# Forward substitution of the 32x32 inverses: from VectorE to GpSimd, its negation and transposed copy to ScalarE

## The chip, the cores and the metric

The kernel runs on one core of a Trainium2 chip. The metric is device time in microseconds of one execution, given as the median of several runs. The core has five engines that work side by side, each through a queue of its own in an order fixed when the kernel is built: TensorE (PE in the profile; PEld is its weight load), VectorE (DVE), ScalarE (ACT), GpSimd (POOL) and SyncE (SP), which issues most of the transfers. They meet at semaphores only.

## The reference, cut to what matters

One layer of a hybrid decoder: 512 prompt tokens and 8 x 8 sampled tokens (576 columns), 1024 channels. After a norm and a combined projection, a Mamba-2 branch and an RWKV-7 branch run side by side; then come an output projection, a SwiGLU block and a gated embedding. The change lies in RWKV-7, whose state obeys, token by token and head by head,

```
s_kk = einsum('bhvk,bhk->bhv', s, kk_t)
s = (s * w_t[:, :, None, :] - s_kk[..., None] * (kk_t * a_t)[:, :, None, :]
     + v_t[..., None] * k_t[:, :, None, :])
out = einsum('bhvk,bhk->bhv', s, r_t)
```

The kernel doesn't step through tokens. It takes 64 tokens as a group; within a group the dependence of each token on the earlier ones is a strictly triangular 64x64 matrix L for each head, and the group is solved with the inverse of (I + L).

## The kernel before

The 576 columns make nine groups of 64 tokens (group 0 holds the sampled tokens). The 16 heads are done in four quarters of four heads. For a quarter, `prep` makes the decayed keys and queries, `gram` makes the triangular matrices (`Lst`) with TensorE and masks them, `solve` and `combine` invert them, `chain` walks through the groups with the 64x64 state, and `head_norm` finishes the output. Quarters overlap: while the chain of one quarter runs, the next is prepared and inverted, and the fourth inverse is traced after the early loads of the Mamba-2 branch.

`solve` (L652 to L679) inverts the two 32x32 diagonal blocks of every 64x64 matrix: 2 blocks x 2 heads of a pair x 18 (9 groups, 2 pairs) = 72 blocks for a quarter. Four transfers (L662) write the blocks of `Lst` to DRAM, one (L665) brings them back as the tile `L`, one block to a partition: 72 partitions x 32 x 32. Then VectorE makes `Tt = -L` (L667), adds 1 on the diagonal (L668) and runs the substitution: for jx = 1 to 30 an outer product of row jx of L with column jx of `Tt` into `tmp` (L674), jx(31-jx) elements a partition, and a subtraction from the rest of `Tt` (L676). L677 writes the transposed copy of the first 36 blocks over `L`. L678 and L679 store `Tt` and the copy to DRAM (`Td`, `Ad`). `combine` loads them in another layout (L688, L690), and with two series of 32x32 matmuls (L698, L712) makes the off-diagonal block, so that the tile `TT` holds the 64x64 inverses. In `chain`, `core` uses `TT` at L797, between two small copies on ScalarE and VectorE (L791/L792 to `xs`, L804/L805 to `suv`); `prompt_state` updates the state at L831.

Beside this stand the projections ("fill"): all weights come in blocks of 128x512 in float32, are loaded by SyncE (L199, tile `raw`, three buffers) and split into a high and a low part, `whi` by ScalarE (L203, shown at the helper's line L93) and `wlo` by a subtraction (L206) that alternates between GpSimd and VectorE; each part has two buffers. TensorE does three products for every block (L221, L222, L223). A projected tile is then evacuated and worked on by ScalarE and VectorE: `shifted` (L368 to L371), `conved` (L395 to L401), `zed` (L411).

The order of each queue is not written by hand in these parts: the framework schedules instructions when the program is closed, by their place in the program text (earlier is more urgent) and a simulated timeline, and writes one fixed order for each engine. A few places are pinned (`issue_after`).

`V`, `S`, `G`, `T` are VectorE, ScalarE, GpSimd and TensorE; `act` is an activation on ScalarE, by default a copy with a scale.

Of the kernel before, what the change touches and what calls it, by code (L numbers as in the profile page):

```python
# [11 lines left out]
ALU = mybir.AluOpType  # L12
# [63 lines left out]
def hybrid_step(ctx, tc, A):  # L76
    nc = tc.nc
    V, S, G, T = nc.vector, nc.scalar, nc.gpsimd, nc.tensor
# [9 lines left out]
    def nm(s):  # L88
        uid[0] += 1
        return f"{s}_{uid[0]}"  # L90

    def act(out, in_, func=AF.Copy, scale=1.0, bias=0.0):
        return S.activation(out, in_, func, bias=bias, scale=scale)  # L93
# [80 lines left out]
    at, n = PV["shift_mu"]  # L174
    V.tensor_scalar(omu[:], pv[:, at:at + n], -1.0, 1.0, ALU.mult, ALU.add)
    hka = const("hka", [P, 16])
    at, n = PV["k_a"]
# [100 lines left out]
    def cslot(name, shape=None, dt=F32):  # L278
        return sp.tile(shape or [P, NT], dt, tag="cv", name=nm(name), bufs=3)
# [372 lines left out]
    def solve(s):  # L652

        q = s.q
        Ld = dp.tile([2, 2, 18, 32, 32], F32, tag=f"Ld{q}", name=f"Ld{q}")
        s.Td = dp.tile([2, 2, 18, 32, 32], F32, tag=f"Td{q}", name=f"Td{q}")
        s.Ad = dp.tile([2, 18, 32, 32], F32, tag=f"Ad{q}", name=f"Ad{q}")
        NB = 72
        for z in range(2):
            for e in range(2):  # L660
                r0 = e * 64 + z * 32
                nc.sync.dma_start(Ld[z, e].rearrange("g s t -> s g t"),  # L662
                                  s.Lst[r0:r0 + 32, :, :, z * 32:z * 32 + 32].rearrange("s g j t -> s (g j) t"))
        L = sp.tile([NB, 32, 32], F32, tag="L", name=nm("L"))
        nc.sync.dma_start(L[:], Ld[:].rearrange("z e g s t -> (z e g) s t"))  # L665
        Tt = s2.tile([NB, 32, 32], F32, tag="Tt", name=nm("Tt"))
        V.tensor_scalar(Tt[:], L[:], -1.0, None, ALU.mult)  # L667
        V.tensor_tensor(Tt[:].rearrange("p s t -> p (s t)")[:, 0:1024:33],  # L668
                        Tt[:].rearrange("p s t -> p (s t)")[:, 0:1024:33], ones[0:NB, 0:32], ALU.add)
        tmp = s2.tile([NB, 256], F32, tag="tmp", name=nm("tmp"))  # L670
        for jx in range(1, 31):
            n = 31 - jx
            o = tmp[:, 0:jx * n].rearrange("p (s t) -> p s t", s=jx)
            V.tensor_tensor(o, L[:, jx:jx + 1, jx + 1:32].to_broadcast([NB, jx, n]),  # L674
                            Tt[:, 0:jx, jx:jx + 1].to_broadcast([NB, jx, n]), ALU.mult)
            V.tensor_tensor(Tt[:, 0:jx, jx + 1:32], Tt[:, 0:jx, jx + 1:32], o, ALU.subtract)  # L676
        V.tensor_copy(L[0:36], Tt[0:36].rearrange("p s t -> p t s"))  # L677
        nc.sync.dma_start(s.Td[:].rearrange("z e g s t -> (z e g) s t"), Tt[:])  # L678
        nc.sync.dma_start(s.Ad[:].rearrange("e g s t -> (e g) s t"), L[0:36])  # L679

# [240 lines left out]
    def inverse(s):  # L921
        solve(s)
        fill_at(s, 7)
        combine(s)
# [331 lines left out]
    for what in SEQ:  # L1256
# [7 lines left out]
        elif what == "y":  # L1264
            for j in range(6):
                t = cslot("yl")
                nc.sync.dma_start(t[:], yr_d[j][:])
                YR.append(split(t[:], xp, ("xhi", "xlo"), [P, NT], lo_eng=G))
        else:
            ps = lin_ps()  # L1270
            linear(YR[0:6], ps)
            t = cslot("pr")
# [71 lines left out]
    def ft(name):  # L1344
        return pools[-1].tile([P, NT], F32, tag="f", name=nm(name), bufs=9 if len(pools) > 1 else 6)
# [31 lines left out]
    for k in range(4):  # L1377
        xa, xb, t = ft("xa"), ft("xb"), ft("tt")
# [100 lines left out]
    for a, b in ((0, 320), (320, NT)):  # L1479
        n = b - a  # L1480
# [17 lines left out]
        for c in range(8):  # L1498
# [14 lines left out]
            t = ft("pg")[:, 0:n]  # L1513
# [159 lines left out]
```

## Time and profile before

| | us |
|---|---|
| median of 3 runs | 1345.34 |
| lowest and highest of them | 1345.02, 1348.39 |
| span of the profiled execution, first to last instruction | 1349.0 |
| PE busy in the span | 1246.8 |
| DVE busy | 826.0 |
| POOL busy | 625.6 |
| ACT busy | 618.9 |

The profiled execution is one by itself; for it the profile gives the span alone, which lies 3.7 us above the median of the runs. In the profile's rows a line begins with the place in the kernel, the engine and the operation, then what is written and read, the shapes (partitions x elements a partition) and the count; after the bar stand the busy time in us, the mean of one in ns, and the idle time of the engine just before, with what ended most of it. In rows by time the first two numbers are the start and the duration in us, and a bracket gives the idle time before and what ended it. Rows of one line give minimum/median/maximum in ns. Matmul records are pipelined, so that their durations overlap.

### The profile page before, as it was taken

The page shows a single profiled execution, that of the slowest core. Times are in us where ns is not written, and L with a number is a line of the kernel's source. Part 1 is how long each engine was busy: PE and PEld are TensorE (multiplying, and loading weights), DVE is VectorE, ACT ScalarE, POOL GpSimd, SP SyncE. Part 2 cuts the span into 40 slices and gives each one's busy share as a digit, 9 for nine tenths or more (in the row PEclk, how much of TensorE's full clock was granted, in tenths as well). Part 3 has the DMA queues.
Part 4 walks back from the last instruction along what each step waited for, and adds up shares of the span by engine and source line. Part 5 has one row for each costly group of instructions (what it writes and reads, how often), then busy time and mean ns, then how long its engine had stood idle before and what let it go on. Part 6 is the DMA issues. An engine that isn't in the chain of part 4 may idle for free.

```text
span 1349.0 us, 26596 instructions
## 1 busy us (share of the span) xinstructions
PE 1246.8 (92%) x10525; PEld 1150.7 (85%) x10525; DVE 826.0 (61%) x1443; ACT 618.9 (46%) x1256; POOL 625.6 (46%) x597
## 2 busy tenths in 40 slices
PE   6897999999989978899999969989999999999997
PEld 6787897889868957788779859889999999999997
DVE  6648666887687785943466667886553135443454
ACT  6565436534654463343434364464442124433363
POOL 5425413642355154122456645565654336654642
PEclk9897799899979978889989989998999999999998
DMA  5322242234232412262454542222323222314322
GB/s 164 125 68 66 77 117 63 85 103 116 75 99 78 109 41 80 94 214 83 157 176 131 179 125 72 73 93 88 92 88 87 79 86 82 93 59 149 96 89 71
DMA packets 94461, 135.58 MB, mean 100 GB/s; under 512 B 34705, under 2 KB 39057, under 8 KB 94337
## 3 DMA queue, kind: packets, MB, share of 16 engines
q1 hardware_dynamic: 93760, 133.36, 32.4%
q8 instruction: 83, 1.36, 0.4%
q10 hardware_dynamic: 576, 0.52, 0.1%
q14 instruction: 42, 0.34, 0.1%
HBM read 106.10 MB, written 27.75 MB: 99 GB/s over the span
## 4 chain that ended last, share of the span: by engine, by line
PE 63%; DVE 14%; ACT 4%; issue 4%; DMA 3%; POOL 3%; DVEq 0%; SPq 0%; ACTq 0%; POOLq 0%
PE lin L234 21%; PE lin L1403 8%; PE lin L223 6%; PE lin L221 6%; PE lin L222 6%; DVE h L395 2%; PE lin L1508 1%; PE lin L1509 1%; PE lin L1510 1%; DVE tmp L674 1%; DVE wlo L206 1%; DVE Tt L676 1%; PE lin L613 1%; PE cx L797 1%; DVE suv L831 1%
## 5 line engine op out<-in xcount | busy, mean ns | idle before, releaser
L206 POOL TENSOR_TENSOR wlo<-raw,whi 128x512 fp32r<-128x512 f32 (+1 forms) x108 | 146.4, 1356 | 352.5 <-ACT whi L93 269.5
L93 ACT ACTIVATE whi<-raw 128x512 fp32r<-128x512 f32 (+1 forms) x232 | 143.3, 618 | 259.1 <-PE lin L234 126.4
L221 PE MATMUL lin<-xhi,whi 128*128 128x288 f32 (+1 forms) x784 | 243.3, 311 | 2.5 <-ACT whi L93 2.2
L223 PE MATMUL lin<-xhi,wlo 128*128 128x288 f32 (+1 forms) x784 | 241.5, 308 | 2.3 <-POOL wlo L206 2.3
L222 PE MATMUL lin<-xlo,whi 128*128 128x288 f32 (+1 forms) x784 | 241.5, 308 | 0.3 <-POOL xlo L194 0.3
L206 DVE TENSOR_TENSOR wlo<-raw,whi 128x512 fp32r<-128x512 f32 (+1 forms) x124 | 100.9, 814 | 103.2 <-PE lin L234 60.4
L221 PEld LDWEIGHTS lin<-xhi,whi 128*128 128x128 f32 (+1 forms) x784 | 151.0, 193 | 9.3 <-ACT whi L93 2.6
L223 PEld LDWEIGHTS lin<-xhi,wlo 128*128 128x128 f32 (+1 forms) x784 | 150.7, 192 | 6.2 <-POOL wlo L206 2.8
L222 PEld LDWEIGHTS lin<-xlo,whi 128*128 128x128 f32 (+1 forms) x784 | 150.8, 192 | 4.8 <-issue 1.2
L234 PE MATMUL lin<-xhi,whi 128*128 128x288 f32 x384 | 62.3, 297 | 3.2 <-ACT xhi L93 3.0
L234 PE MATMUL lin<-xlo,whi 128*128 128x288 f32 x384 | 60.8, 298 | 0.0
L234 PE MATMUL lin<-xhi,wlo 128*128 128x288 f32 x384 | 59.3, 297 | 0.0
L234 PEld LDWEIGHTS lin<-xhi,whi 128*128 128x128 f32 x384 | 54.6, 189 | 3.8 <-ACT xhi L93 1.7
L234 PEld LDWEIGHTS lin<-xlo,whi 128*128 128x128 f32 x384 | 54.8, 191 | 0.0
L234 PE MATMUL lin<-ah,wlo 128*128 128x288 f32 x352 | 54.7, 296 | 0.0
L234 PE MATMUL lin<-al,whi 128*128 128x288 f32 x352 | 54.7, 296 | 0.0
L234 PE MATMUL lin<-ah,whi 128*128 128x288 f32 x352 | 54.7, 296 | 0.0
L234 PEld LDWEIGHTS lin<-xhi,wlo 128*128 128x128 f32 x384 | 54.3, 191 | 0.0
L1403 PE MATMUL lin<-T,wh 128*128 128x288 f32 x320 | 50.1, 296 | 4.5 <-DVE T L194 2.8
L674 DVE TENSOR_TENSOR tmp<-L,Tt 72x30 f32<-72x30 f32 (+14 forms) x120 | 49.2, 410 | 3.2
L234 PEld LDWEIGHTS lin<-ah,whi 128*128 128x128 f32 x352 | 49.6, 189 | 0.0
L234 PEld LDWEIGHTS lin<-ah,wlo 128*128 128x128 f32 x352 | 49.6, 189 | 0.0
(425 smaller groups left out, 3197.8 us busy)
## 6 DMA issues: line engine op xcount, KB each, us to landing
raw<-wts SPq DMA_DIRECT2D x271, 256.0 KB, 2.6
S<-s_wkv SPq DMA_DIRECT2D x8, 512.0 KB, 5.1
hd<-s_ssm SPq DMA_DIRECT2D x8, 512.0 KB, 4.5
o_ssm_s<-hd SPq DMA_DIRECT2D x8, 512.0 KB, 2.9
xbc_d<-E SPq DMA_DIRECT2D x12, 288.0 KB, 2.1
x<-xT SPq DMA_DIRECT2D x8, 288.0 KB
gate_d<-g SPq DMA_DIRECT2D x8, 288.0 KB, 2.5
bv_d<-rw SPq DMA_DIRECT2D x8, 288.0 KB
```

Of the source, the lines that this page charges most:

```text
L93: return S.activation(out, in_, func, bias=bias, scale=scale)
L206: eng.tensor_tensor(lo[:, 0:n], raw[:, 0:n], hi[:, 0:n].bitcast(F32), ALU.subtract)
L221: T.matmul(ps[:, a:b], whi, xhi[:, a:b], start=first, stop=False)
L222: T.matmul(ps[:, a:b], whi, xlo[:, a:b], start=False, stop=False)
L223: T.matmul(ps[:, a:b], wlo, xhi[:, a:b], start=False, stop=last)
L234: T.matmul(ps[:, a:e], (hi, lo)[p][:, i * P:(i + 1) * P], xs[k + i][q][:, a:e], start=n == k + i == 0, stop=n == 2 and k + i == nk - 1, sk ...
L395: V.scalar_tensor_tensor(h[:], E[:, i:i + 600], w(i), h[:], ALU.mult, ALU.add)
L613: T.matmul(ps[:, c:c + 128].rearrange("p (a t) -> p a t", a=2), s.BK[jj][H[e], g].rearrange("p a t -> p (a t)"), s.G[H[e], g, jj, :, e], s ...
L674: V.tensor_tensor(o, L[:, jx:jx + 1, jx + 1:32].to_broadcast([NB, jx, n]), Tt[:, 0:jx, jx:jx + 1].to_broadcast([NB, jx, n]), ALU.mult)
L676: V.tensor_tensor(Tt[:, 0:jx, jx + 1:32], Tt[:, 0:jx, jx + 1:32], o, ALU.subtract)
L797: T.matmul(uw[H[e], jj, :], TT[H[e], g, jj, :], xs[H[e], jj, :], start=True, stop=True)
L1403: T.matmul(ps, (hi, lo)[p][:, k * P:(k + 1) * P], OPS[n][k][q], start=first and p == q == k == 0, stop=p == 1 and k == 3, skip_group_check ...
```

## The change

The negation L667 and the transposed copy L677 become activations on ScalarE, and the addition on the diagonal (L668) and the sixty operations of the substitution (L674, L676) are issued on GpSimd, in all four quarters. The arithmetic, the tiles and the transfers are as before.

```diff
         Tt = s2.tile([NB, 32, 32], F32, tag="Tt", name=nm("Tt"))
-        V.tensor_scalar(Tt[:], L[:], -1.0, None, ALU.mult)
-        V.tensor_tensor(Tt[:].rearrange("p s t -> p (s t)")[:, 0:1024:33],
+        act(Tt[:], L[:], scale=-1.0)
+        G.tensor_tensor(Tt[:].rearrange("p s t -> p (s t)")[:, 0:1024:33],
                         Tt[:].rearrange("p s t -> p (s t)")[:, 0:1024:33], ones[0:NB, 0:32], ALU.add)
         tmp = s2.tile([NB, 256], F32, tag="tmp", name=nm("tmp"))
         for jx in range(1, 31):
             n = 31 - jx
             o = tmp[:, 0:jx * n].rearrange("p (s t) -> p s t", s=jx)
-            V.tensor_tensor(o, L[:, jx:jx + 1, jx + 1:32].to_broadcast([NB, jx, n]),
+            G.tensor_tensor(o, L[:, jx:jx + 1, jx + 1:32].to_broadcast([NB, jx, n]),
                             Tt[:, 0:jx, jx:jx + 1].to_broadcast([NB, jx, n]), ALU.mult)
-            V.tensor_tensor(Tt[:, 0:jx, jx + 1:32], Tt[:, 0:jx, jx + 1:32], o, ALU.subtract)
-        V.tensor_copy(L[0:36], Tt[0:36].rearrange("p s t -> p t s"))
+            G.tensor_tensor(Tt[:, 0:jx, jx + 1:32], Tt[:, 0:jx, jx + 1:32], o, ALU.subtract)
+        act(L[0:36], Tt[0:36].rearrange("p s t -> p t s"))
```

## The prediction

> **What bounds the kernel now.** I read the page's busy shares first, then one row for each of the four stretches in which an inverse is computed, then TensorE's idle gaps inside those stretches, and last the durations on GpSimd (POOL) and VectorE (DVE).
>
> ```profile
> span 1349.0 us, 26596 instructions
> PE 1246.8 (92%) x10525; PEld 1150.7 (85%) x10525; DVE 826.0 (61%) x1443; ACT 618.9 (46%) x1256; POOL 625.6 (46%) x597
> ```
>
> TensorE (PE) is busy 92% of the span, so the time is what PE must do plus what it loses; the change saves no matmul. The next rows are the windows from the negation L667 to the transposed copy L677 of quarters 0 to 3; after the window come its length and the busy time of PE, weight loads, DVE, ACT and POOL, then the granted clock.
>
> ```profile
> 146.70:186.90 40.20, 40.20 (x296) 38.47 (x295) 36.49 (x84) 15.88 (x33) 8.90 (x11) 0.97 0.27 79
> 276.20:321.60 45.40, 43.06 (x352) 39.84 (x352) 43.24 (x104) 14.76 (x34) 13.03 (x19) 0.96 0.30 91
> 418.30:458.80 40.50, 38.30 (x325) 35.77 (x324) 38.12 (x99) 13.84 (x35) 8.75 (x10) 0.96 0.26 77
> 536.50:574.40 37.90, 33.74 (x268) 28.53 (x267) 34.82 (x95) 11.65 (x27) 5.75 (x7) 0.84 0.28 90
> ```
>
> The reader is to see three things. DVE is full in every window (36.49 of 40.20, and so on), and POOL nearly empty. Yet PE is full too, because projections are laid into the window: in quarter 0 it loses nothing at all. So a full DVE is no proof that DVE costs time; only PE's gaps are. Here are the four gaps of over 1 us that touch the inverse; the bracket gives the idle time and what ended it.
>
> ```profile
> 192.83 0.24 PE L698 MATMUL cx<-AA,Lst 32*32 32x32 f32 x2 [1.34 <-DMA AA<-Ad]
> 280.84 0.38 PE L797 MATMUL cx<-xs,TT 64*64 64x64 f32 x5 [2.34 <-DVE xs L792]
> 422.23 0.58 PE L789 MATMUL cx<-suv,G 128*128 128x128 f32 x2 [2.20 <-DVE suv L831]
> 562.58 0.79 PE L789 MATMUL cx<-suv,G 128*128 128x128 f32 x2 [2.85 <-DVE suv L831]
> ...
> 420.00:440.00 20.00, 17.80 (x141) 17.09 (x140) 18.75 (x54) 6.30 (x17) 3.15 (x5) 0.91 0.31 98
> ```
>
> In the last three, a small DVE instruction of the previous quarter's chain stands in DVE's queue behind the inverse. A gap also costs clock: the slice with the second of them was granted 0.91, that is 20 x 0.09 = 1.8 us of matmul time. DVE itself had been held at the head of its queue by the load of L, 12.2 us in three times:
>
> ```profile
> DVE Tt L667 <- DMA L<-Ld: 12.2, 3, 5.0
> ```
>
> **Part 1: what DVE loses.** All four inverses:
>
> ```profile
> L674 DVE TENSOR_TENSOR tmp<-L,Tt 72x30 f32<-72x30 f32 (+14 forms) x120 | 49.2, 410 | 3.2
> L676 DVE TENSOR_TENSOR Tt<-Tt,tmp 72x30 f32<-72x30 f32 (+14 forms) x120 | 45.2, 377 | 3.4
> ...
> L667 DVE TENSOR_SCALAR Tt<-L x4: 690/1456/1979, 146.7 to 536.5; 72x1024 f32<-72x1024 f32 x4
> ...
> L677 DVE COPY L<-Tt x4: 1068/1092/1111, 185.7 to 573.3; 36x1024 f32<-36x1024 f32 x4
> ```
>
> 49.2 + 45.2 + about 4 x 1.4 + 4 x 1.1 = 104 us leave DVE, 26 us a quarter. Its worth is only PE's gaps: at most 2.34 + 2.20 + 2.85 = 7.4 us, and 1.8 us of clock at each of the first two, 3.6: together 11.0 us. The gap at 192.83 does not go, since it waits for the inverse itself. The low end is 0, because the 12.2 us of waiting for L move to ACT (the negation) and to POOL behind it (L668 needs the negation), and ACT carries the chain's `xs`, `suv` and `bkt` copies and every `whi`. I take 5 us, a little under half: before 280.84 the wait for L began with DVE and ACT both inside the chain, so one holder replaces the other, but the queue behind L667 on DVE held sixty more instructions and the queue on ACT will not.
>
> **Part 2: what GpSimd takes.** Per quarter 60 operations: for jx = 1 to 30 a product and a subtraction of jx(31-jx) elements, 4960 elements for each kind. Prices (minimum/median/maximum, then a group's count, busy time and mean):
>
> ```profile
> L1429 POOL TENSOR_TENSOR e<-e,e x10: 797/812/1262, 915.1 to 1200.8; 128x288 f32<-128x288 f32 x10
> ...
> L1434 POOL TENSOR_TENSOR e<-e,e x10: 806/1256/1267, 923.1 to 1210.5; 128x288 f32<-128x288 f32 x10
> ...
> L846 POOL TENSOR_TENSOR um<-suv,dmb x16: 1039/1090/1611, 218.7 to 616.8; 128x512 f32<-128x512 f32 x16
> ...
> L638 POOL TENSOR_TENSOR G<-G,gmask x32: 661/667/677, 133.8 to 533.3; 64x256 f32<-64x256 f32 x32
> L638 POOL TENSOR_TENSOR G<-G,dgmask x8: 420/424/501, 132.1 to 513.1; 64x128 f32<-64x128 f32 x8
> ...
> L206 POOL TENSOR_TENSOR wlo<-raw,whi 128x512 fp32r<-128x512 f32 x103 | 142.7, 1386 | 346.2 <-ACT whi L93 263.2 <-PE lin L234 32.0 <-ACT ar L93 15.4
> ```
>
> From 424 ns at 128 and 667 ns at 256 elements: 1.90 ns an element and 0.18 us fixed; I use 0.195 us. The dense form L1429, fastest 797 ns at 288, gives (797-195)/288 = 2.09 ns for the subtraction; L846, which repeats both operands as the product does, fastest 1039 ns at 512, gives 1.65 ns. So 60 x 0.195 + 4960 x (1.65 + 2.09) ns = 11.7 + 18.6 = 30.3 us, and 0.3 us for the diagonal L668: 30.6 us a quarter where DVE spent (49.2 + 45.2)/4 = 23.6. No row has instructions this small in long dependent series: the fixed part may be 0.1 us dearer (36.6 us) or, overlapped, 0.1 cheaper (24.6).
>
> The ratio for the same 128x512 split is 1386 ns on POOL against 681 on DVE (below). The Trainium skill, GPSIMD Engine Reference, section 3.1, gives 4497 ns against 2293 for two inputs of 2048 elements, 1.96 times; by that the 23.6 us would become an estimated 46 us instead of 30.6, which is the third rival's size; on the dense split the trace agrees with the ratio, on small shapes no row here shows it.
>
> **Part 3: what the two engines do to each other.** DVE first, then POOL, at the same times:
>
> ```profile
> 284.30 1.43 DVE L674 TENSOR_TENSOR tmp<-L,Tt 72x184 f32<-72x184 f32 x1
> 285.76 0.36 DVE L676 TENSOR_TENSOR Tt<-Tt,tmp 72x184 f32<-72x184 f32 x1
> ...
> 284.24 1.29 POOL L206 TENSOR_TENSOR wlo<-raw,whi 128x512 fp32r<-128x512 f32 x1 [6.59 <-ACT whi L93]
> ...
> 141.63 0.76 DVE L598 TENSOR_TENSOR rw<-lin,rw 128x576 f32<-128x576 f32 x1 [0.92 <-PE lin L246]
> ...
> 141.51 3.74 POOL L650 TENSOR_TENSOR bk<-bk,pc 128x1024 f32<-128x1024 f32 x2
> ```
>
> A DVE instruction with both inputs in SBUF, started inside a POOL one, ends 0.2 us after it: 1.43 us instead of 0.36. One with an input in PSUM (L598) runs through at 0.76. So from now on each two-SBUF-input DVE instruction in a window holds up POOL's series. The main ones, window by window (two, three, one and two rows):
>
> ```profile
> L206 DVE TENSOR_TENSOR wlo<-raw,whi 128x512 fp32r<-128x512 f32 x4 | 2.7, 681 | 0.0
> L395 DVE SCALAR_TENSOR_TENSOR h<-E,hw,h 128x600 f32<-128x600 f32 x3 | 2.5, 827 | 0.0
> ...
> L395 DVE SCALAR_TENSOR_TENSOR h<-E,hw,h 128x600 f32<-128x600 f32 x6 | 5.0, 832 | 0.0
> L206 DVE TENSOR_TENSOR wlo<-raw,whi 128x512 fp32r<-128x512 f32 x5 | 3.4, 680 | 0.0
> L400 DVE SCALAR_TENSOR_TENSOR E<-th,h 128x512 f32<-128x512 f32 x2 | 1.4, 680 | 0.0
> ...
> L206 DVE TENSOR_TENSOR wlo<-raw,whi 128x512 fp32r<-128x512 f32 x4 | 2.7, 681 | 0.0
> ...
> L411 DVE SCALAR_TENSOR_TENSOR hz<-thz,hz 128x576 f32<-128x576 f32 x3 | 2.2, 749 | 0.0
> L206 DVE TENSOR_TENSOR wlo<-raw,whi 128x512 fp32r<-128x512 f32 x3 | 2.0, 681 | 0.0
> ```
>
> 5.2, 9.8, 2.7 and 4.2 us. The Trainium skill, SBUF — State Buffer, section "SBUF: two separate sides", says the pair of ports is locked by whichever starts first and for the whole instruction, and names DVE instructions with two SBUF inputs; the 1.43 us agree.
>
> POOL's need is then its old work + 30.6 + these: 44.7, 53.4, 42.1 and 40.6 us, against windows of 40.2, 45.4, 40.5 and 37.9: an excess of 4.5 + 8.0 + 1.6 + 2.7 = 16.8 us. Where it lands is the open question. As a later inverse it is mostly covered: in quarter 1 the last load of AA was issued at 326.5 and its first matmul ran at 341.9.
>
> ```profile
> 326.51 1.49 SPq L690 DMA_DIRECT2D AA<-Ad  x1
> ...
> L698 PE MATMUL cx<-AA,Lst x4: 191/202/212, 341.9 to 342.0; 32*32 32x32 f32 x4
> ...
> 170.66 0.63 ACT L93 ACTIVATE whi<-raw 128x512 fp32r<-128x512 f32 x1
> 171.37 1.47 POOL L206 TENSOR_TENSOR wlo<-raw,whi 128x512 fp32r<-128x512 f32 x1 [5.26 <-ACT whi L93]
> ```
>
> The weight splits are not covered. Every second `wlo` is POOL's; it now stands between inverse operations in a queue whose order is fixed beforehand. Today it starts 0.1 us after its `whi` (171.37 after 170.66 + 0.63) and takes 1.3 to 1.5. With two `whi`/`wlo` buffers, a split begins when PE has left a block and must end before PE has done the next: 24 matmuls (4 row blocks, 2 halves, 3 products) at the 40.20/296 = 0.136 us of the quarter-0 window, 3.3 us. Take off 0.63 for `whi`, 1.5 for `wlo` and some 0.4 for hand-overs (an estimate), and 0.8 us are left. A wait for one inverse operation (30.6/60 = 0.5) fits; two do not. So excess POOL work reaches PE through late `wlo`, split after split, and behind it SP's load of the next `raw` into the freed buffer. Between 0 (the order leaves room) and 16.8 us I take two thirds, 11 us, because PE is full just where the excess is largest.
>
> **Part 4: what ACT takes.** Two activations a quarter; DVE's 1.09 us for the transposed copy and ACT's 629 ns at 512 elements put each near 1.1 us. ACT has 15.88 of 40.20 us in use, so 0 on the path, up to 8 x 1.1 = 9 if each delays a `whi`. The two stores L678 and L679 stay on SP, now released by POOL and ACT; `raw` loads queue behind them as before: 0.
>
> ```profile
> L93 ACT ACTIVATE whi<-raw 128x512 fp32r<-128x512 f32 x221 | 138.8, 629 | 243.8 <-PE lin L234 112.3 <-PE lin L222 75.6 <-issue 40.2
> ```
>
> **The sum.** -5 (DVE's queue) + 11 (POOL's excess) + 0 (ACT) = +6 us against the profiled span of 1349.0, which lies 3.7 us over the median of the runs, 1345.34. I put it on the median: 1351 us, 0.4% slower.
>
> **The rivals.** First, *the queue is freed and POOL is hidden* (faster): no `wlo` comes late, the three gaps and their clock go: 1345.3 - 11.0 = 1334 us. For it: POOL's use of 8.90 in 40.20 us, and 12 us between inverse and use in quarter 1. Against: it needs POOL's order to be right within 0.8 us at all its splits in the windows; it turns into the forecast as soon as two inverse operations stand ahead of a split. Second, *both cancel*: POOL's excess reaches PE with a third, 5.6 us, against 5 gained: 1346. Third, *POOL becomes the bound*: L1434 runs 806 ns alone and 1256 at the median of the same shape, 1.56 times; if the inverse's operations are stretched so, 30.6 becomes 47.7 us, the excess (with old work, without the list above) 16.4 + 15.3 + 16.0 + 15.6 = 63 us, two thirds of it 42, less 5: 1382 us. For it: a dependent series under constant company; against: DVE's company shrinks by 26 us a quarter. Fourth, *ACT takes over the wait for L*: the gaps stay, nothing is gained, +11: 1356 us.
>
> **How the numbers follow.** Forecast 0.32, fourth rival 0.06, third 0.12: slower by over 0.3% 0.50. Second rival 0.20: within 0.3%, about 4 us, what a measurement of this kernel tells from no change. First rival, with smaller gains on the same side, 0.30: faster. The range takes in most of the first rival and half of the third: 1336 to 1378 us, with 0.1 left out on each side; the forecast's own is 1347 to 1362 us.
>
> **What would show it.** In the changed profile: DVE near 720 us busy and POOL near 750; inverse operations on POOL of 0.2 to 0.7 us, about 31 us a quarter; the first of them waiting for ACT's negation, which waits for L; the gaps behind L792 and L831 gone; and PE, in the four windows, waiting at L223 for POOL's `wlo`, most in quarters 0 and 1. If the windows show PE full and those waits absent, part 3 is wrong; if an inverse takes 45 us and more of POOL time, part 2 is; if `whi` comes late behind the negation, the wait for L was only handed on.

## The result, and the profile after

The changed kernel has a median of 1355.8 us over eight runs (1351.7 to 1365.2), the kernel before 1346.3 us over the eight runs beside them (1336.7 to 1348.4). The ratio is 1.0081, 95% interval 1.0055 to 1.0106: slower by 0.8%, some 11 us. The profiled execution of the changed kernel took 1355.56 us and has a span of 1353.9 us, against 1349.0 before. The 1349.0 is more than the slowest of those eight runs of before, so the two profiles differ by 4.9 us where the medians differ by 9.5. All comparisons by time below therefore use the runs, and the profiles serve to find places. One execution of one kernel below, the profiled one of the change in quarter 0 alone, ran at a mean clock of 0.73 and took 1512 us; it is left out, and that kernel's trace isn't read.

The head of the page, of the changed kernel:

```profile
span 1353.9 us, 26612 instructions
PE 1245.4 (92%) x10525; PEld 1149.5 (85%) x10525; DVE 746.5 (55%) x1191; ACT 628.1 (46%) x1262; POOL 755.1 (56%) x841
```

TensorE has the same 10525 matmuls and the same busy time. 80 us have left VectorE, 130 us have come to GpSimd. The four windows of the inverses, now from ScalarE's negation to its transposed copy, with the same columns as in the prediction (length, busy time of PE, weight loads, DVE, ACT and POOL, then the granted clock):

```profile
145.30:197.60 52.30, 50.80 (x382) 48.66 (x381) 18.30 (x29) 23.41 (x44) 44.09 (x73) 0.98 0.28 84
283.00:332.00 49.00, 45.43 (x387) 42.06 (x387) 23.53 (x46) 19.42 (x45) 44.76 (x78) 1.00 0.29 87
425.00:474.00 49.00, 47.72 (x417) 43.90 (x411) 18.85 (x45) 18.60 (x46) 42.59 (x75) 1.00 0.27 85
543.00:588.00 45.00, 39.73 (x321) 34.73 (x320) 16.64 (x31) 16.36 (x35) 37.16 (x68) 0.85 0.26 80
```

The full column has moved from DVE to POOL, and the windows, which took 38 to 45 us before, take 45 to 52 now. POOL has 83 to 91% of each window in use and PE, as before, is nearly full. The costs on POOL, in the page's groups:

```profile
L676 POOL TENSOR_TENSOR Tt<-Tt,tmp 72x30 f32<-72x30 f32 (+14 forms) x120 | 67.7, 564 | 8.7
L674 POOL TENSOR_TENSOR tmp<-L,Tt 72x30 f32<-72x30 f32 (+14 forms) x120 | 66.3, 553 | 7.8
```

The two instructions on ScalarE (count, then minimum/median/maximum in ns), and behind them its wait at the negation between 100 and 700 us:

```profile
L93 ACT ACTIVATE Tt<-L x4: 1060/1061/1063, 145.3 to 542.7; 72x1024 f32<-72x1024 f32 x4
L93 ACT ACTIVATE L<-Tt x4: 2078/2092/2104, 195.5 to 586.7; 36x1024 f32<-36x1024 f32 x4
```

```profile
ACT Tt L93 <- DMA L<-Ld: 20.8, 4, 5.4
```

A quarter of 67.7 + 66.3 is 33.5 us, and the last column says that POOL stood idle another 8.7 + 7.8 = 16.5 us just before these operations, 4.1 us a quarter: 65 to 73 ns on average lie between one operation and the next that needs it. A quarter thus holds POOL for 37.6 us and not for 30.6.

Now TensorE's waits from 100 to 700 us, of the kernel before and then of the changed one (us in all, times, longest):

```profile
PE cx L789 <- DVE suv L831: 6.6, 4, 2.9
PE cx L797 <- DVE xs L792: 6.3, 4, 2.8
...
PE lin L223 <- POOL wlo L206: 2.3, 3, 1.1
```

```profile
PE lin L223 <- POOL wlo L206: 9.8, 8, 3.0
PE cx L797 <- DVE xs L792: 5.7, 4, 2.5
PE cx L789 <- DVE suv L831: 3.8, 3, 1.9
```

The late splits cost 7.5 us more; the two waits behind VectorE's queue cost 3.4 us less, and the waits behind VectorE as a whole only 0.5 us less (21.3 and 20.8). All waits of PE in this stretch, summed over the rows of that view, are 51.4 us before and 59.4 after. The longest one behind a split, at 295.83, can be followed through POOL, DVE, ACT and PE in the timeline (start, duration):

```profile
287.90 0.63 ACT L93 ACTIVATE whi<-raw 128x512 fp32r<-128x512 f32 x1 [1.15 <-POOL tmp L674]
...
289.69 0.47 POOL L676 TENSOR_TENSOR Tt<-Tt,tmp 72x150 f32<-72x150 f32 x1
290.24 1.09 POOL L674 TENSOR_TENSOR tmp<-L,Tt 72x168 f32<-72x168 f32 x1
291.41 1.20 POOL L676 TENSOR_TENSOR Tt<-Tt,tmp 72x168 f32<-72x168 f32 x1
292.68 0.93 POOL L674 TENSOR_TENSOR tmp<-L,Tt 72x184 f32<-72x184 f32 x1
293.69 0.87 POOL L676 TENSOR_TENSOR Tt<-Tt,tmp 72x184 f32<-72x184 f32 x1
294.52 1.26 POOL L206 TENSOR_TENSOR wlo<-raw,whi 128x512 fp32r<-128x512 f32 x1
295.74 0.53 POOL L674 TENSOR_TENSOR tmp<-L,Tt 72x198 f32<-72x198 f32 x1
...
291.35 1.90 DVE L395 SCALAR_TENSOR_TENSOR h<-E,hw,h 128x600 f32<-128x600 f32 x2
293.17 0.99 DVE L206 TENSOR_TENSOR wlo<-raw,whi 128x512 fp32r<-128x512 f32 x1
...
292.47 0.63 ACT L93 ACTIVATE whi<-raw 128x512 fp32r<-128x512 f32 x1 [2.15 <-PE lin L222]
...
295.83 0.40 PE L223 MATMUL lin<-xhi,wlo 128*128 128x288 f32 x1 [3.00 <-POOL wlo L206]
```

The splits alternate, so the `whi` of 292.47 belongs to VectorE's split at 293.17, and POOL's split belongs to the `whi` before it, which is ready at 288.53. The split on POOL could begin there, but seven operations of the inverse start ahead of it, between 288.67 and 293.69. The last four run beside VectorE instructions with two SBUF inputs and take 0.87 to 1.20 us, where the one of 150 elements before them took 0.47 and the one of 198 behind the split 0.53. The split starts at 294.52, 6.0 us late; PE has nothing left from 292.83 on, and stands for 3.00 us. This is the kind of wait that part 3 of the prediction described, with other sizes: the room was 2.9 us here (from 288.53 to PE's need at 292.67, less 1.26 for the split) and not 0.8, and seven operations stood in it, not two.

The inverse of quarter 0 ends later, and so does what needs it. Its combine began at 192.83 before (the row in the prediction); in the changed kernel:

```profile
195.53 2.09 ACT L93 ACTIVATE L<-Tt 36x1024 f32<-36x1024 f32 x1 [1.33 <-POOL Tt L676]
...
202.64 0.31 PE L698 MATMUL cx<-AA,Lst 32*32 32x32 f32 x2 [1.71 <-DMA AA<-Ad]
```

9.8 us later. And one cost that no row of waits shows, the clock. Three windows of 3.41 us behind one another in the changed kernel (length, PE busy; the granted clock is the third number from the end), and matmuls of one shape from the second and the third:

```profile
199.05:202.46 3.41, 1.89 (x36) 1.63 (x34) 1.71 (x4) 2.47 (x3) 0.58 (x1) 1.00 0.53 86
202.46:205.87 3.41, 3.23 (x14) 3.17 (x15) 0.68 (x3) 0.39 (x4) 0.00 (x0) 0.50 0.82 212
205.87:209.28 3.41, 3.41 (x80) 3.21 (x79) 0.68 (x1) 0.34 (x1) 0.00 (x0) 1.00 0.39 150
```

```profile
204.01 0.44 PE L222 MATMUL lin<-xlo,whi 128*128 128x288 f32 x1
204.25 0.44 PE L223 MATMUL lin<-xhi,wlo 128*128 128x288 f32 x1
...
206.04 0.29 PE L222 MATMUL lin<-xlo,whi 128*128 128x288 f32 x1
206.18 0.30 PE L223 MATMUL lin<-xhi,wlo 128*128 128x288 f32 x1
```

PE was busy for 55% of the first window, and in the next the clock is halved: matmuls of one shape follow each other every 0.24 us, and every 0.13 to 0.14 us in the third window. (The counts of the windows don't compare: most of the 80 records are small 32x32 matmuls.) The twelve of them in the second window came an estimated 12 x 0.107 = 1.3 us later for it, on top of the wait of 1.71 us. Every drop in this trace and in that of before has this form: half the clock, for a multiple of 3.41 us, except where the last one is cut off by the end.

Each run's span can thus be put into two parts: span x (mean clock), called the time at full clock below, and span x (1 - mean clock), counted as lost to the clock. The means over the changed kernel's eight runs are 1275.6 and 79.3 us. For the eight runs of before beside them only the times are known; over 23 runs of before in a later comparison the means are 1272.0 and 70.1 us (standard deviations 2.7 and 4.4). The split assumes that everything slows with the clock, and it doesn't. Added up over the half-clock stretches of the changed kernel's profile, 161.5 us, PE is idle for 30.2 of them. And among the runs of before, in the three sets of the experiments, a run with 1 us more in the lost part is only 0.53 to 0.66 us longer. What is counted as lost is therefore an upper bound, by an estimate from these runs nearly twice the price. Of the 12.8 us between the means, 9.2 are counted as lost and an estimated 5 to 6 are clock; the rest, about 7, is near the 8.0 us by which PE's waits differ. In the two profiles the lost part is the same, 81 us each.

### The profile page after: what moved, and what is told of

Its sections match the earlier page's. It is cut to its first block, busy times and chain, and to the rows that moved or that the text cites. A ratio compares the mean times of both kernels' runs of the same rounds, so it can differ in the third digit from the quotient of the medians.

```text
span 1353.9 us, 26612 instructions
## 1 busy us (share of the span) xinstructions
PE 1245.4 (92%) x10525; PEld 1149.5 (85%) x10525; DVE 746.5 (55%) x1191; ACT 628.1 (46%) x1262; POOL 755.1 (56%) x841
## 4 chain that ended last, share of the span: by engine, by line
PE 59%; DVE 13%; POOL 7%; ACT 4%; DMA 4%; issue 4%; SPq 0%; DVEq 0%; POOLq 0%; ACTq 0%
PE lin L234 21%; PE lin L1403 8%; PE lin L223 6%; PE lin L221 6%; PE lin L222 6%; POOL Tt L676 2%; POOL tmp L674 2%; DVE h L395 2%; PE lin L613 1%; DMA raw<-wts 1%; DMA L<-Ld 1%; DVE wlo L206 1%; ACT G L93 1%; PE cx L812 1%; PE cx L789 1%
## 5 line engine op out<-in xcount | busy, mean ns | idle before, releaser
L206 POOL TENSOR_TENSOR wlo<-raw,whi 128x512 fp32r<-128x512 f32 (+1 forms) x108 | 143.2, 1326 | 236.7 <-ACT whi L93 158.6
L223 PE MATMUL lin<-xhi,wlo 128*128 128x288 f32 (+1 forms) x784 | 242.4, 310 | 10.2 <-POOL wlo L206 9.8
L206 DVE TENSOR_TENSOR wlo<-raw,whi 128x512 fp32r<-128x512 f32 (+1 forms) x124 | 106.2, 857 | 138.7 <-ACT whi L93 68.0
L223 PEld LDWEIGHTS lin<-xhi,wlo 128*128 128x128 f32 (+1 forms) x784 | 150.8, 193 | 16.9 <-POOL wlo L206 11.6
L676 POOL TENSOR_TENSOR Tt<-Tt,tmp 72x30 f32<-72x30 f32 (+14 forms) x120 | 67.7, 564 | 8.7
L674 POOL TENSOR_TENSOR tmp<-L,Tt 72x30 f32<-72x30 f32 (+14 forms) x120 | 66.3, 553 | 7.8
```

Of the source, the lines that this page charges most:

```text
L206: eng.tensor_tensor(lo[:, 0:n], raw[:, 0:n], hi[:, 0:n].bitcast(F32), ALU.subtract)
L223: T.matmul(ps[:, a:b], wlo, xhi[:, a:b], start=False, stop=last)
L674: G.tensor_tensor(o, L[:, jx:jx + 1, jx + 1:32].to_broadcast([NB, jx, n]), Tt[:, 0:jx, jx:jx + 1].to_broadcast([NB, jx, n]), ALU.mult)
L676: G.tensor_tensor(Tt[:, 0:jx, jx + 1:32], Tt[:, 0:jx, jx + 1:32], o, ALU.subtract)
```

## The experiments

The theories. One, *late splits*: POOL's `wlo` stands behind the inverse's operations, and PE waits at L223. Two, *the later inverse*: quarter 0's combine has nothing to cover it. Three, *ScalarE*: the negation holds ScalarE's queue while it waits for `L`, and the copy is slow. Four, *the order written anew*: with an edit the framework can write another fixed order for all queues, and the time follows the new order rather than any one operation. PE's instructions in the traces, neighbours of one line and one pair of tiles taken as one, make 4444 rows before; a comparison of rows finds 387 that differ where only the two ScalarE instructions are moved, 107 for the negation alone and 22 for the copy alone. Each kernel was timed in five rounds against before, whose median was 1343.4 to 1343.7 us in the three sets. All at a glance, in us against before's means, with the two parts just described (for the changed kernel, before's are the 23 later runs):

| kernel | ratio, 95% | at full clock | counted as lost |
|---|---|---|---|
| changed | 1.0081 [1.0055, 1.0106] | +3.6 | +9.2 |
| negation and copy back on VectorE | 1.0312 [1.0278, 1.0347] | +18.1 | +24.2 |
| only negation and copy on ScalarE | 1.0095 [1.0061, 1.0129] | -4.9 | +17.5 |
| changed, all `wlo` on VectorE | 1.0135 [1.0101, 1.0168] | +6.1 | +12.4 |
| before, all `wlo` on VectorE | 1.0014 [0.9994, 1.0035] | -3.3 | +5.2 |
| change in quarter 0 alone | 1.0126 [1.0100, 1.0153] | +6.3 | +8.9 |
| change in quarters 1 to 3 alone | 1.0050 [1.0029, 1.0072] | -0.9 | +6.3 |
| only the negation on ScalarE | 1.0039 [1.0022, 1.0056] | -1.6 | +6.0 |
| only the copy on ScalarE | 0.9996 [0.9976, 1.0016] | +0.1 | -1.0 |
| half the substitution, on GpSimd | 1.0079 [1.0051, 1.0108] | +6.2 | +4.1 |
| half the substitution, on VectorE | 0.9965 [0.9949, 0.9982] | +0.2 | -4.9 |
| before, `L` of quarter 0 delayed | 1.0064 [1.0039, 1.0089] | +6.3 | +2.2 |
| before, `L` of quarters 1 to 3 delayed | 1.0184 [1.0154, 1.0214] | +4.3 | +19.2 |

**The two parts of the edit.** First the changed kernel with the two ScalarE instructions put back:

```
-        act(Tt[:], L[:], scale=-1.0)
+        V.tensor_scalar(Tt[:], L[:], -1.0, None, ALU.mult)
...
-        act(L[0:36], Tt[0:36].rearrange("p s t -> p t s"))
+        V.tensor_copy(L[0:36], Tt[0:36].rearrange("p s t -> p t s"))
```

> The substitution stays on GpSimd; the negation and the transposed copy go back to VectorE. Theory 1 (late splits: GpSimd has too much to do in the windows, and TensorE waits at L223 for its wlo): little changes, 0.4 to 1.0% slower than before, waits of PE at L223 for POOL's wlo near 8 to 10 us up to 700 us. Theory 2 (later inverse: the inverse ends 7 to 10 us later and what is laid out behind it opens gaps): as theory 1. Theory 3 (ScalarE: its wait for L, 20.8 us in four, and its copies of 2.09 us hold up whi): at least half of the loss is gone, 0 to 0.4% slower.

1384.3 us, 3.1% over before, the worst of all and beyond what any theory gave. PE's longest waits in it:

```profile
PE lin L223 <- POOL wlo L206: 9.5, 7, 2.7
PE cb L1037 <- DMA dt<-dt_d: 7.9, 1, 7.9
PE lin L223 <- DVE wlo L206: 5.2, 2, 3.7
...
PE cx L698 <- DMA AA<-Ad: 4.4, 4, 2.0
```

The late splits are the same as in the changed kernel. New are a transfer of the Mamba-2 branch (7.9 us), which SyncE issues at 603.14, a microsecond behind the store of quarter 3's `Tt` at 602.13, and VectorE's own late splits: VectorE carries no substitution here, but waits again for `L` (12.7 us in three times) and for the end of the substitution (2.2 us). Then the reverse, the kernel before with these two instructions alone on ScalarE (the same diff read upward, applied to before):

> The substitution stays on VectorE as before; only the negation and the transposed copy are on ScalarE. Theory 3: most of the loss is there, 0.4 to 1% slower than before. Theories 1 and 2: within 0.3% of before, since GpSimd takes nothing and the inverse ends within 2 us of its old time.

1356.5 us, as theory three had it: without moving the substitution at all, this costs as much as the whole change. Its two waits on the negation, and PE's at the splits:

```profile
ACT Tt L93 <- DMA L<-Ld: 17.7, 4, 5.4
DVE Tt L668 <- ACT Tt L93: 13.3, 4, 4.2
...
PE lin L223 <- POOL wlo L206: 3.2, 4, 1.1
```

The splits are not late. PE's waits sum to 48.8 us, less than before's 51.4; 17.5 us more are counted as lost to the clock, an upper bound as said. One place is the stretch from quarter 2's combine to the inverse of quarter 3, where PE is not full in any of these kernels (47 to 52 of 60 us). Before and then this kernel, 470 to 530 us:

```profile
470.00:530.00 60.00, 46.95 (x561) 35.84 (x560) 43.20 (x84) 34.96 (x81) 27.45 (x32) 0.83 0.15 49
```

```profile
470.00:530.00 60.00, 51.58 (x531) 39.21 (x532) 41.88 (x73) 31.90 (x70) 25.25 (x29) 0.69 0.23 72
```

PE is idle for 4.6 us less (60 - 51.58 against 60 - 46.95), but it has done some 30 matmuls fewer, at a clock lower by 0.14, at most 0.14 x 60 = 8.4 us. A sum of waits, taken alone, would have called this kernel the faster one. The two profiles differ by 1.9 us in span, so they show a place where clock is lost, not where all of the 13 us between the medians went.

**Late splits.** The changed kernel with all `wlo` of the projections on VectorE from the first quarter's start to the last chain's end, and the same in the kernel before as a control:

```
+    only[0] = V
     for s in Q:
...
     chain(Q[3])
+    only[0] = None
```

> The changed kernel, with all wlo splits of the projections from the first quarter to the end of the fourth chain on VectorE instead of every second one on GpSimd. Theory 1: PE's waits at L223 for POOL's wlo go from 9.8 us to under 1 us and the loss with them: -0.2 to +0.3% of before. Theory 2: GpSimd's inverse gets faster too (some 6 us a quarter less other work), so part of the loss goes, but new gaps stay: 0.3 to 0.6% slower. Theory 3: no change, 0.8% slower.

> The kernel before with the same splits all on VectorE: the control for e3. VectorE is full in the windows already (36 of 40 us) and gets 3 to 5 splits of 0.68 us more in each: the inverse ends 3 us later and splits come late; all theories expect 0.3 to 1.5% slower than before, with PE's waits at L223 now for DVE's wlo. If it is no slower, e3 says nothing on the change.

The control costs next to nothing (1344.8 us), where all theories had expected 0.3 to 1.5%: in the kernel before, VectorE can do all splits. The last sentence of the expectation, that a control which is no slower says nothing on the change, has it the wrong way round: it is because the control is no slower that the other kernel can be read, with the reserve that VectorE has POOL's series beside it there. In the changed kernel POOL's late splits are gone, and yet it is at 1360.8, no better than with them:

```profile
PE cx L698 <- DMA AA<-Ad: 5.9, 3, 4.8
PE lin L223 <- DVE wlo L206: 4.9, 5, 2.1
...
PE lin L221 <- ACT whi L93: 3.6, 2, 1.9
```

The wait moved to VectorE's splits, to ScalarE's `whi` and to the inverse itself. Late splits are real, but taking them away doesn't bring the time back; theory one doesn't account for the loss alone. No theory had given 1.35% for this kernel.

**Which quarters.** The whole change in some quarters only; the others as before:

```
+        E = G if q == 0 else V        # or: q > 0
-        act(Tt[:], L[:], scale=-1.0)
+        if E is G:
+            act(Tt[:], L[:], scale=-1.0)
+        else:
+            V.tensor_scalar(Tt[:], L[:], -1.0, None, ALU.mult)
...
-            G.tensor_tensor(Tt[:, 0:jx, jx + 1:32], ...
+            E.tensor_tensor(Tt[:, 0:jx, jx + 1:32], ...
```

> The whole change (substitution on GpSimd, negation and copy on ScalarE) in quarter 0 alone; quarters 1 to 3 as before. Against before: later inverse of quarter 0, nothing covers it (theory 2): +6 to +10 us, first combine near 202 instead of 193 us. Late splits (theory 1): +2 to +4. ScalarE's two activations (theory 3): about a quarter of the +13 of the kernel that moved these alone, +3. The order written anew (theory 4): no rule, anything from -5 to +10, with the first combine not the place where the loss arises.

> The whole change in quarters 1 to 3 alone; quarter 0 as before. Against before: theory 2: 0 to +3 us, since behind quarter 0 an inverse has slack, and VectorE's 78 us less may even gain up to 11. Theory 1: +6. Theory 3: +8 to +10, as the two activations cost +13 when moved alone in all four quarters and their loss arose in quarters 2 and 3. Theory 4: anything from -5 to +13.

Quarter 0 alone costs 1.26% (five runs from 1356.4 to 1363.3), more than any theory had given, the other three together 0.5%, and all four 0.8%. That quarter 0 weighs more than the three others is what theory two says; that quarter 0 alone is no cheaper than all four is what no theory of separate costs can give. In quarters 1 to 3 the splits are as late as in the changed kernel,

```profile
PE lin L223 <- POOL wlo L206: 10.3, 8, 3.1
```

and the waits on VectorE, summed over all rows, fall from 21.3 to 14.4 us, so that all of PE's waits sum to 51.4 us, as before: here the exchange that the prediction put into its sum can be seen, 8.0 against 6.9 us. What else makes this kernel 7 us slower shows in no wait; 6.3 us are counted as lost to the clock.

**The two ScalarE instructions apart.** The kernel before with one of them on ScalarE, the other on VectorE:

> Before, with the negation alone on ScalarE in all quarters; substitution and transposed copy on VectorE. Theory 3: the wait for L at the head of ScalarE's queue (17.7 us in four where both moved) is the cost: +9 to +13 us. Theory 2: the negation is no longer on ScalarE than on VectorE, 0 to +2. Theory 4: anything from -4 to +13, unrelated to the next kernel's result.

> Before, with the transposed copy alone on ScalarE in all quarters. Theory 3 (the wait for L held by ScalarE): 0 to +2 us, since the negation stays on VectorE. Theory 2: the copy takes 2.1 us where VectorE took 1.1, quarter 0 pays 1 us: +1 to +2. Theory 4: anything from -4 to +13; the sum of this and the kernel with the negation alone then isn't the +13 of both together.

The negation costs 0.4%, the copy nothing, although it takes 2.1 us where VectorE took 1.1; both together cost 0.95%. ScalarE's wait for `L` at the negation is 20.7 us in four times when the negation moves alone, so that wait by itself doesn't cost 0.95%. The sign of theory three is right for the negation, its size isn't, and the two don't add up.

**Half the substitution.** `for jx in range(1, 31, 2)`, in the changed kernel and in the one before: the even steps are left out.

> The change, with only the odd jx of the substitution (30 of its 60 operations for a quarter; the even steps are left out). GpSimd then has about 17 us a quarter instead of 34, and the inverse of quarter 0 is done near 178 us instead of 195. If the length of the inverse is what costs (theory 2), it is now shorter than before's 37 us and the loss is gone: 1338 to 1344 us. If GpSimd's load and its late splits cost in proportion (theory 1): about half of the +10, 1348. If the two activations on ScalarE with their waits cost, whoever does the substitution (theory 3): still 1352 to 1356. Order written anew (theory 4): 1340 to 1356.

> Before, with the same half of the substitution left out, on VectorE: 12 us a quarter leave VectorE and the inverse is some 15 us shorter. Theory 2: the start of quarter 0's combine comes earlier: 1330 to 1338 us. If neither VectorE's load nor the inverse's length was worth anything before: 1343 +- 3. The difference to the half on GpSimd is what the place of the work costs at half size.

This pair says most. On VectorE the half saves 0.35%, less than theory two had given for a combine that comes 21.1 us earlier. On GpSimd it saves next to nothing against the whole: 1354.3 us, 0.79% over before, which is what theory three had forecast (the wide range of theory four takes it in too), and theories one and two had not. PE's longest waits, and the first combine in the timeline:

```profile
PE lin L223 <- POOL wlo L206: 8.2, 8, 2.3
PE cx L797 <- ACT xs L93: 7.0, 4, 3.7
```

```profile
178.34 0.24 PE L698 MATMUL cx<-AA,Lst 32*32 32x32 f32 x2
```

Quarter 0's combine comes 14.5 us earlier than before, and the kernel is slower all the same: theory two is no sufficient cause. By the starts of the combines in the two profiles, the lead is 13.2 us in quarter 1 and 4.0 in quarter 2, and in quarter 3 a lag of 7.4 has come of it. The kernel with the two ScalarE instructions alone has the same shape: 0.4 to 2.3 us ahead in quarters 0 to 2, and 6.0 behind in quarter 3. Both lose between quarter 1's combine and quarter 3's, where the half on VectorE keeps 13.1 of its lead of 21.1 us. What the two share is the ScalarE pair; that it is the cause, and by which of its waits, no run here shows. The splits cost 8.2 us with half of the operations, against 9.8 with all: theory one's wait is there, but it isn't in proportion to POOL's work. The place of the substitution costs 1354.3 - 1339.7 = 14.6 us at half size, where it costs 9.5 at full size (the ScalarE pair moves with it both times).

**A later inverse without engine work.** In the kernel before, `L` goes to DRAM and back once more ahead of the negation:

```
+        if q == 0:                    # or: q > 0
+            Lb = dp.tile([NB, 1024], F32, ...)
+            nc.sync.dma_start(Lb[:], L[:]...)
+            nc.sync.dma_start(L[:]..., Lb[:])
```

> Before, with the tile L of quarter 0 sent to DRAM and back once more ahead of the negation (two transfers of 288 KB): no engine gets more work, the inverse of quarter 0 comes about 5 us later. Theory 2 (quarter 0 has no cover): +4 to +8 us. If a later inverse is covered: 0 to +1. Theory 4: anything from -4 to +13.

> Before, with the same detour of L in quarters 1 to 3 and none in quarter 0: three inverses come about 5 us later. Theory 2: covered behind quarter 0, 0 to +2 us. If lateness costs wherever it falls: +8 to +15 us. Theory 4: anything from -4 to +13.

The detour delays the negation of quarter 0 by 5.3 us and its first combine by 4.5, and costs 0.64%, a little over what theory two had given. In quarters 1 to 3 the negations start 4.3, 10.9 and 8.0 us later than before, and the kernel costs 1.84%, 23.5 us and more than any theory had given; 19.2 us are counted as lost to the clock. The first combines of quarters 1, 2 and 3 in that kernel start at 341.20, 484.45 and 597.16, against

```profile
341.92 0.76 PE L698 MATMUL cx<-AA,Lst 32*32 32x32 f32 x36
...
479.81 0.88 PE L698 MATMUL cx<-AA,Lst 32*32 32x32 f32 x43
...
588.43 0.80 PE L698 MATMUL cx<-AA,Lst 32*32 32x32 f32 x22
```

before. Quarter 1 is covered; 2 and 3 pass the delay on, 4.6 and then 8.7 us. So "covered behind quarter 0" is true of quarter 1 alone. The test is not pure. The two transfers stand in SyncE's queue, and loads of weights behind them wait too. And VectorE is held by it: the negation stands at the head of its queue until `L` comes, in this kernel for 22.1 us where before it was 12.2, and the two late splits here start right behind a held negation, at 281.24 and 545.14.

```profile
DVE Tt L671 <- DMA L<-Lb: 22.1, 3, 8.0
...
PE lin L223 <- DVE wlo L206: 5.9, 2, 3.1
```

So part of the 1.84% is an engine held by the wait for `L`, which theory three says of ScalarE, and not the lateness of the inverse.

## Why the prediction was right, and which of its steps were not

The forecast was 1351 us, 5.7 us over the 1345.3 that it was made against, by -5 for VectorE, +11 for late splits and 0 for ScalarE. Measured were 1355.8 against 1346.3, +9.5. The direction held, and the late splits, its largest term, are there; that they are what makes the kernel slower is not shown. The steps fared as follows.

*Part 1, VectorE's queue: -5 us.* VectorE lost 80 us instead of 104, since its remaining instructions with two SBUF inputs now stand against POOL's (746.5 busy, where 720 was named): the 33 or 34 splits on VectorE from 140 to 600 us have a mean of 673 ns before and 862 ns after. Of the three gaps named, those at 280.84 and 422.23 are gone and that at 562.58 fell from 2.85 to 1.15 us: 6.2 of the 7.4 us. But others grew, as the one of 1.92 us at 255.99 (0.86 before), so that PE's waits at L797 and L789 fell by only 3.4 us, and waits behind VectorE as a whole by 0.5. The gain was there in the kernel with quarters 1 to 3 (6.9 us), and mostly lost again in the changed one: 5 was too much by 2 to 4. The clock counted with the first two gaps did come back at its place: the windows of quarters 1 and 2 were granted 0.96 before and 1.00 in the changed kernel. Over the whole span the two profiles lost the same, 81 us.

*Part 2, the price on POOL: 30.6 us a quarter.* Mis-sized, 33.5 busy and 37.6 with the 65 to 73 ns between dependent operations, just above the upper bound of 36.6. The smallest operation took 232 ns, close to the 0.195 + 30 x 1.65 = 0.24 us of the formula, so the fixed part was right; the rest is, at least in part, stretching beside VectorE (0.87 to 1.20 us in the rows shown). The doubling of VectorE's price, an estimated 46 us, did not come.

*Part 3, late splits: +11 us.* The wait is shown: four kernels with operations of the substitution on POOL (all, those with the ScalarE part put back, quarters 1 to 3, half of them) wait 8.2 to 10.3 us at L223 for POOL's `wlo`, seven with none there, and the splits shared as before, 1.2 to 3.2. That is +7.5 us in the changed kernel, where 11 stood in the sum. The size came from the wrong model. It took an excess of POOL's need over its window, 16.8 us, and passed two thirds on; with half of the operations there is no such excess, and the wait is 8.2 us. That fits a wait set by which operations the fixed order puts ahead of a split, and by how far VectorE stretches them, more than by the length of the series; it is read from the one split followed above. The room of 0.8 us was wrong too where it was followed: 2.9 us, with seven operations in it. "Most in quarters 0 and 1" is half true: the longest, 3.00 us, is in quarter 1, but quarters 2 and 3 have 1.19 and 1.47 beside quarter 0's 1.50. The other sentence of this part, that a later inverse is mostly covered, was drawn from quarter 1's 12 us of slack. It holds there, and not in quarter 0, which goes to its combine at once; in 2 and 3 the kernel with the delayed `L` passed the delay on.

*Part 4, ScalarE: 0.* This step failed. The negation took 1.06 us as estimated, the transposed copy 2.09 instead of 1.1, and the wait for `L` went over whole, 20.8 us in four times where VectorE had 12.2. The two alone make the kernel without the rest 0.95% slower, 13 us, over the bound of 9 that the prediction gave. The price is not that of a delayed `whi` (PE waits 0.7 us for one there), and no wait of PE shows it; part of it is clock.

*What the sum had no term for.* The clock appears in the prediction only as a gain. Of the 12.8 us between the means, an estimated 5 to 6 are clock, with before's runs from another set. That the sum came near is partly luck: +6 stands against +8.0 of waits in the profiles (59.4 - 51.4) because the splits were put 3.5 us too high and the gain 2 to 4 us too high, and the two errors cancel; the rest of the 9.5 lies among ScalarE's price and the clock, both at nothing in the sum.

Of the rivals, the one in which ScalarE takes over the wait for `L` gave 1356; the number fits, and its reason, that the gaps behind VectorE stay, is partly seen: the named ones shrink by 6.2 us, and others open. "POOL becomes the bound" is excluded by the halved kernel and by PE's windows of 0.88 to 0.97 busy.

What stays open is which moved instruction brings which part of the loss. Quarter 0 alone costs as much as all quarters, negation and copy together more than the sum of both, and half of the substitution as much as the whole. Theory four would allow all of that, but the size of a new order doesn't set its price: all `wlo` of before on VectorE changes 1462 rows of PE's order and costs 0.14%, the ScalarE pair 387 and costs 0.95%. No run held the order still while an operation changed, and an edit without any content was not run. Nor did any run put the negation on GpSimd with the substitution, where no other engine would be held by the wait for `L`. No kernel tried that computes everything is faster than before: the best is the copy on ScalarE at 0.9996 [0.9976, 1.0016].

## What to carry to other kernels

A long dependent series on an engine that also feeds TensorE can cost by the feeds that stand behind it more than by its own length: here the waits behind it were 9.8 us with the whole series and 8.2 with half of it. An engine that is full but covered is no reason to move work; ask first which waits of TensorE end at it (here 12.9 us before, 9.5 after). To move an instruction that waits for a transfer moves its wait into another queue (`L`: 12.2 us on VectorE before, 20.8 on ScalarE). And where TensorE is nearly full, look at the granted clock of every run before any wait is explained: a kernel with fewer waits can be the slower one. Ask of the runs what a microsecond counted as lost to the clock is worth; here it was about 0.6 us.

## What the runs showed of the hardware

The clock of TensorE fell to half in steps of 3.41 us, at which 128x288 matmuls followed each other every 0.24 us and not every 0.13, and it didn't take an idle window: in the changed kernel 14 of 17 drops follow a 3.41 us window in which PE was busy for 0 to 61%, the one shown 55%, while some windows with 48 to 70% led to none. The Trainium skill, "TensorE: Matmul & The Clock Gate", Part 1, gives a free-running window of 3413 ns and two states, half and full clock, and the traces shown agree; its condition for the fall, a whole idle window, is not what is seen here.

Runs of one kernel differ in this clock: over 23 runs of before the mean clock runs from 0.940 to 0.952, span x (1 - clock) has a standard deviation of 4.4 us, and a run with 1 us more of it is 0.56 us longer.

A copy that transposes 36 x 32 x 32 elements inside a partition took 2.09 us on ScalarE and 1.09 on VectorE; the dense negation of 72 x 1024 took 1.06 on ScalarE. VectorE's split of a 128x512 block took 673 ns on average before and 862 ns beside GpSimd's series (140 to 600 us).
